# Where the split weights begin in SBUF: 64 instead of 128 bytes modulo 256

## The chip, the cores and the metric

The kernel runs on one core of a Trainium2 chip. The metric is the device time of one execution in microseconds (us). TensorE (PE in the profile) multiplies a *standing* operand, loaded ahead by a weight load of its own (PEld), with a *moving* operand that streams through it column by column. VectorE is DVE, ScalarE is ACT, GpSimd is POOL, SyncE is SP. The operands of TensorE lie in SBUF, 128 partitions wide; what this document calls a place is the byte address within a partition, taken modulo 256.

## The reference, cut to what matters

One decoder layer on 256 tokens with a width of 1024, all in float32:

```
h = RMSNorm(x);  proj = h @ w_in           # q, k/v of three branches, gates, MoBA q/k/v, merge gates
y_A = native sparse attention(proj);  y_B = block-sparse attention(proj)
x = x + (sig(g_A) * (y_A @ w_up_nsa) + sig(g_B) * (y_B @ w_up_moba)) @ w_out
x = x + relu(RMSNorm(x) @ w_ff1)**2 @ w_ff2
out = RMSNorm(x)
```

`w_in` has 4888 columns, `w_ff1` is 1024 x 4096 and `w_ff2` is 4096 x 1024, so nearly all the work is matrix products with weights that are read once.

## The kernel before

**Chunks.** All weights come as 60 chunks of at most 128 x 2048 float32 (`CHUNKS`, L20): the four of k/v (`kva`, `kvb`, whose pieces are 384 and 408 columns), eight of q and MoBA q/k/v, eight of the merge gates (`gm`), four of the up projections, four of `wout`, 16 of `ff1` and 16 of `ff2`. SyncE loads a chunk into a `raw` tile.

**Split.** `split` (L102) makes two tiles of a chunk: `whi` is the chunk rounded to the fast format `float32r` (ACT, L114), `wlo` is the rest `raw - whi` (DVE, L116). Activations are split the same way (`hTh`/`hTl`, `yTh`/`yTl`, `mxh`/`mxl`, `h2h`/`h2l`, `sqh`/`sql`). A product is then three matmuls (`mm3`, L240): high by high, high by low, low by high, added up in PSUM. The pool `wp` holds three buffers each of `raw`, `whi` and `wlo`; a buffer comes free when the last matmul that reads it is done.

**Which operand stands.** `xstat` (L245) lets the activations stand and the weights move, mostly 512 columns at a time; the input projection uses it. The up projections and `ff2_mms` (L955) do the same. `wstat` (L260) lets the weights stand and moves the activations, 256 columns at a time; `wout` and `ff1` use it. So the same buffers `whi` and `wlo` serve as moving operands in one stage and as standing ones in another.

**ff2 by seven products.** For the six chunks in `SEVEN` the four block products of `ff2` are replaced by seven products of sums (`seven_mms`, L968). Sums of weight blocks are formed by DVE in the `raw` tile (`t_sums`, L887) and split into `th` and `tl` (`t_hi`, `t_lo`), which move; sums of activations (`sh`, `sl`, `sxh`, `sxl`) stand.

**The order.** It is written out by hand: `run_slot` (L223) emits the matmuls of a slot and, at given shares of it, the splits, loads, evacuations and attention steps of that slot. The engines run their queues in this order and wait for each other by semaphores.

**Places.** Every buffer has a fixed place that follows from the sizes of the tiles allocated before it; some tiles are only there as gaps, and some operands are slices that begin a few elements into their tile. In the kernel before, the places modulo 256 are these:

| product | moving operand, place | standing operand, place | columns that move |
|---|---|---|---|
| kva | whi/wlo, 128 | hT, 128 | 384 |
| kvb, pieces 0 to 3 of a chunk | whi/wlo, 128, 224, 64, 160 | hT, 128 | 408 |
| q, qm, km, vm, gm | whi/wlo, 128 | hT, 128 | 512 |
| up projections | whi/wlo, 128 | yT, 128 | 512 |
| wout | mx, 64 | whi/wlo, 128 | 256 |
| ff1 | h2, 64 | whi/wlo, 128 | 256 |
| ff2 | whi/wlo, th/tl, 128 | sq, s, sx, 128 | 512 |
| ff2, last 24 matmuls | whi/wlo, 128 | sq, 128 | 256 |

The pieces of a kvb chunk are 408 x 4 = 1632 bytes apart, which is why they have four places; all other pieces are multiples of 256 bytes.

Of the kernel before, what the change touches and what calls it, by code (L numbers as in the profile page):

```python
# [9 lines left out]
F32R = mybir.dt.float32r  # L10
# [22 lines left out]
C_Q, C_QM, C_KM, C_VM, C_GM, C_UPN, C_UPM, C_WOUT, C_FF1, C_FF2 = (  # L33
    4, 6, 8, 10, 12, 20, 22, 24, 28, 44)
# [7 lines left out]
def hybrid_layer(ctx: ExitStack, tc: tile.TileContext, firstd, gxd, w, w1c, small, const, gf, out):  # L42
# [4 lines left out]
    wp = ctx.enter_context(tc.tile_pool(name="wp", bufs=3))  # L47
# [36 lines left out]
    raw, hi, lo = {}, {}, {}  # L84

    def seven(c):
        return c >= C_FF2 and c - C_FF2 in SEVEN

    def raw_tile(c):
        raw[c] = wp.tile([128, 2048], F32, name="raw")  # L90

# [5 lines left out]
    def load(c):  # L97
        if c < NCH:
            raw_tile(c)
            load_part(c, 0, 1)  # L100

    def split(c, part, parts=2, which=""):  # L102
        if c >= NCH:
            return
        n = CHUNKS[c][2]
        if part == 0 and c not in hi:
            hi[c] = wp.tile([128, 2048], F32R, name="whi")
            lo[c] = wp.tile([128, 2048], F32R, name="wlo")
        a, b = part * n // parts, (part + 1) * n // parts
        if seven(c):  # L110
            a, b = ((0, 512), (1024, 2048))[part]
        v = raw[c][:, a:b] if c else raw0[:, part]
        if which != "l":
            act.activation(hi[c][:, a:b], v, AF.Copy)  # L114
        if which != "h":
            dve.tensor_tensor(lo[c][:, a:b], v, hi[c][:, a:b].bitcast(F32),  # L116
                              op=ALU.subtract)
# [39 lines left out]
    for k in range(4):  # L157
        c0, c1 = (16 + 640 * k if k else 0), 16 + 640 * k + 640
        nc.sync.dma_start(g0x[:, c0:c1], firstd[:, c0:c1])
    raw_tile(1)  # L160
    arrived(0, raw[1])
    load_part(1, 0, 1)
    arrived(1, gx[:, 16 + 1024:])
    load_x(16 + 1024, 16 + 2048)
    raw_tile(2)
    arrived(2, raw[2])
    load_part(2, 0, 1)
# [17 lines left out]

    def act_pair(name, o):
        return (cp.tile([128, 2048 + e], F32R, name=name + n, tag="act" + n.upper())[:, o:o + 2048]
                .rearrange("p (k q) -> p k q", k=8) for n, e in (("h", 128), ("l", 16)))

    hTh, hTl = act_pair("hT", 16)  # L190

    def h_part(kt):
# [77 lines left out]
    def split_events(c, hs, ls):  # L270
        for i in range(2):
            at(hs[i], split, c + 2, i, 2, "h")
        for i in range(2):
            if ls[i] <= 1:
                at(ls[i], split, c + 2, i, 2, "l")
        if ls[1] <= 1 and not seven(c + 2):
            at(max(ls) + 0.05, load, c + 5)
# [304 lines left out]
    for kt in range(4):  # L582
        h_part(kt)
        split(0, kt, 4)
# [36 lines left out]
    for sec, c0, n in groups:  # L621
# [6 lines left out]
        for i in range(2):  # L628
            c = c0 + i
# [57 lines left out]
    for g in range(4):  # L687
        accs = [acc_tile(), acc_tile()]
        for i in range(2):
            c = C_GM + 2 * g + i  # L690
# [9 lines left out]


    mxh, mxl = act_pair("mx", 0)

    def upn_evac(t, i, acc):
# [26 lines left out]
    for sec, c0, kind, evac in (("upn", C_UPN, "n", upn_evac), ("upm", C_UPM, "m", upm_evac)):  # L731
        for i in range(2):
            c = c0 + i
# [44 lines left out]
    FB = {}  # L778
# [45 lines left out]
    for i in range(4):  # L824
        c = C_WOUT + i
# [33 lines left out]
    SS, TT = {}, {}  # L859
# [6 lines left out]
    def s_sums(i, r):  # L866
        if not SS:
            FB["p"].tile([128, 40], F32, name="gap3")
            for n, e in (("h", 128), ("l", 16)):
                SS[n] = cp.tile([128, 2048 + e], F32R, name="s" + n, tag="act" + n.upper())  # L870
                SS[n + "x"] = FB["p"].tile([128, 384], F32R, name="sx" + n)
        j = SEVEN.index(i)
        for n in "hl":
            SS[i, n] = (SS[n][:, 16 + 384 * j:400 + 384 * j] if j < 5 else SS[n + "x"])
        S = [FB["scr"][:, 128 * a:128 * a + 128] for a in range(4)]
        A = [[r[:, k, 128 * t:128 * t + 128] for k in range(2)] for t in range(2)]
        for o, x, y, op in ((0, A[1][0], A[1][1], ALU.add), (2, A[0][0], A[1][0], ALU.subtract),
                            (1, S[0], A[0][0], ALU.subtract), (3, A[0][1], S[1], ALU.subtract)):
            dve.tensor_tensor(S[o], x, y, op=op)
# [13 lines left out]
    def t_hi(c, a):  # L893
        if a == 0:
            for n in "hl":
                TT[n] = FB["p"].tile([128, 2176 if n == "h" else 2096], F32R, name="t" + n, tag="h2" + n)[:, 0:2048]
        v = slice(1024 * a, 1024 * a + 1024)
        act.activation(TT["h"][:, v], raw[c][:, v], AF.Copy)  # L898

# [6 lines left out]
    def ff1_evac(i, outs, whole):  # L906
        r = FB["p"].tile([128, 2, 256], F32, name="ur", bufs=2)
        rf = r.rearrange("p a q -> p (a q)")
        h, l = (FB[n][:, 2 * i:2 * i + 2, :].rearrange("p a q -> p (a q)") for n in ("sqh", "sql"))
        if whole is None:  # L910
            for m in range(2):
                act.activation(r[:, m], outs[m], AF.Relu)
        else:
            act.activation(rf, whole, AF.Relu)
        dve.tensor_tensor(rf, rf, rf, op=ALU.mult)
        act.activation(h, rf, AF.Copy)  # L916
        dve.tensor_tensor(l, rf, h.bitcast(F32), op=ALU.subtract)  # L917
        if i in SEVEN:
            s_sums(i, r)
# [8 lines left out]
    for i in range(16):  # L928
        c = C_FF1 + i
# [112 lines left out]
    for i in range(15):  # L1042
        c = C_FF2 + i
# [8 lines left out]
        if i + 2 in SEVEN:  # L1052
            at(0.62, t_sums, c + 2)
            at(0.65, t_hi, c + 2, 0)
            at(0.66, t_hi, c + 2, 1)
# [116 lines left out]
```

## Time and profile before

| | |
|---|---|
| time, median of 2 runs | 376.62 us (376.49 to 376.75) |
| span of the profiled execution, first to last instruction | 374.1 us |
| time outside the span (difference of the two) | 2.5 us |
| mean granted TensorE clock | 0.997 |
| PE, matmuls in the span | 365.5 us busy, 2388 records |
| DVE / ACT busy | 294.9 us / 219.9 us |
| HBM read | 65.47 MB |

The views used below are: the page itself; the table by stretches (for each stretch of the span its length, and the busy time of each engine with the number of instructions); the chain of waits (the work that ended last, in order of time: start, length, what); the groups of instructions; and the timeline (start, length, engine, line, operation, output and inputs, shape). In a row of the timeline a matmul's length includes its way through the array, which overlaps the next one; the *pace*, from one start to the next, is what counts for time.

### The profile page before, as it was taken

The numbers are of one execution on the slowest core, as the hardware profiler recorded it, in microseconds if no ns is written. First come the engines' busy times: TensorE is split into PE (matmuls) and PEld (weight loads), VectorE is DVE, ScalarE is ACT, GpSimd is POOL, SyncE is SP. The second block draws the span as 40 slices with busy tenths as digits, with TensorE's granted clock in tenths as the row PEclk, the third lists the DMA queues.
The fourth block names the chain that finished last, engine by engine and source line by source line (L and its number), as shares of the span: only waits on it lengthen the run. The fifth ranks groups of instructions, "written<-read, shape, count | busy, mean of one in ns | idle before, by whom it ended". The sixth has DMA issues, their size and how long they took to land.

```text
span 374.1 us, 6002 instructions
## 1 busy us (share of the span) xinstructions
PE 365.5 (98%) x2388; PEld 320.9 (86%) x2388; DVE 294.9 (79%) x476; ACT 219.9 (59%) x383; POOL 6.1 (2%) x18
## 2 busy tenths in 40 slices
PE   8999999999999999999999999999999999999993
PEld 7987778878888788778999999999998888888883
DVE  4878888896966869766867688787778879999685
ACT  6966465767747667344455566666664785555412
POOL 2020000000000000000000000000000000000000
PEclk9999999999999999999999999999999999999998
DMA  8996445334533335550675556556655535655202
GB/s 278 366 380 249 142 182 197 112 114 127 189 135 115 112 122 192 155 207 1 223 286 190 185 190 217 156 191 226 209 153 201 203 136 163 231 199 207 100 0 112
DMA packets 10539, 66.89 MB, mean 179 GB/s; under 512 B 1168, under 2 KB 1680, under 8 KB 3216
## 3 DMA queue, kind: packets, MB, share of 16 engines
q1 hardware_dynamic: 10080, 65.61, 50.1%
q10 hardware_dynamic: 432, 0.92, 0.6%
q8 instruction: 18, 0.29, 0.3%
q14 instruction: 9, 0.07, 0.1%
HBM read 65.47 MB, written 1.05 MB: 178 GB/s over the span
## 4 chain that ended last, share of the span: by engine, by line
PE 83%; DVE 7%; ACT 4%; DMA 3%; issue 2%; POOL 1%; SPq 0%; POOLq 0%; ACTq 0%; DVEq 0%
PE acc L238 53%; PE o L238 13%; PE P L238 4%; PE qacc L238 3%; PE yb L238 2%; DVE wlo L116 2%; ACT whi L114 2%; DMA raw<-in_kva_dram 2%; DMA g0x<-in_first_dram 1%; DVE x L988 1%; PE Sa L529 1%; PE Sb L529 1%; PE Sa L238 1%; PE Sb L238 1%; PE tp L319 1%
## 5 line engine op out<-in xcount | busy, mean ns | idle before, releaser
L114 ACT ACTIVATE whi<-raw 128x1024 fp32r<-128x1024 f32 (+3 forms) x124 | 118.4, 984 | 53.2 <-PE acc L238 33.7
L116 DVE TENSOR_TENSOR wlo<-raw,whi 128x1024 fp32r<-128x1024 f32 (+3 forms) x124 | 136.2, 1130 | 13.6 <-ACT whi L114 13.5
L238 PE MATMUL acc<-h2h,whi 128*128 128x256 f32 x256 | 70.7, 276 | 0.0
L238 PE MATMUL acc<-h2l,whi 128*128 128x256 f32 x256 | 70.7, 276 | 0.0
L238 PE MATMUL acc<-h2h,wlo 128*128 128x256 f32 x256 | 70.7, 276 | 0.0
L238 PE MATMUL acc<-whi,hTh 128*128 128x512 f32 (+1 forms) x128 | 51.0, 399 | 0.2 <-DVE kml L338 0.2
L238 PE MATMUL acc<-wlo,hTh 128*128 128x512 f32 (+1 forms) x128 | 50.7, 396 | 0.0
L238 PE MATMUL acc<-whi,hTl 128*128 128x512 f32 (+1 forms) x128 | 49.7, 388 | 0.0
L238 PEld LDWEIGHTS acc<-h2h,whi 128*128 128x128 f32 x256 | 48.0, 188 | 0.0
L238 PEld LDWEIGHTS acc<-h2l,whi 128*128 128x128 f32 x256 | 48.0, 188 | 0.0
L238 PEld LDWEIGHTS acc<-h2h,wlo 128*128 128x128 f32 x256 | 48.0, 188 | 0.0
L238 PE MATMUL o<-whi,sqh 128*128 128x512 f32 (+1 forms) x86 | 33.1, 385 | 0.0
L238 PE MATMUL o<-whi,sql 128*128 128x512 f32 (+1 forms) x86 | 33.0, 384 | 0.0
L238 PE MATMUL o<-wlo,sqh 128*128 128x512 f32 (+1 forms) x86 | 33.0, 384 | 0.0
L238 PEld LDWEIGHTS acc<-whi,hTh 128*128 128x128 f32 x128 | 24.3, 190 | 6.6 <-issue 1.3
L238 PEld LDWEIGHTS acc<-whi,hTl 128*128 128x128 f32 x128 | 24.3, 190 | 4.2
L238 PEld LDWEIGHTS acc<-wlo,hTh 128*128 128x128 f32 x128 | 24.3, 190 | 4.1 <-DVE wlo L116 0.3
L898 ACT ACTIVATE th<-raw 128x1024 fp32r<-128x1024 f32 x12 | 12.7, 1062 | 19.2 <-DVE raw L891 19.2
L917 DVE TENSOR_TENSOR sql<-ur,sqh 128x512 fp32r<-128x512 f32 x16 | 11.1, 693 | 11.2 <-ACT sqh L916 11.2
L238 PEld LDWEIGHTS o<-whi,sql 128*128 128x128 f32 x86 | 16.2, 188 | 3.2
L238 PEld LDWEIGHTS o<-wlo,sqh 128*128 128x128 f32 x86 | 16.2, 188 | 3.2
L238 PEld LDWEIGHTS o<-whi,sqh 128*128 128x128 f32 x86 | 16.1, 188 | 3.1
(318 smaller groups left out, 645.2 us busy)
## 6 DMA issues: line engine op xcount, KB each, us to landing
raw<-in_ff_dram SPq DMA_DIRECT2D x32, 1024.0 KB, 4.9
raw<-in_gm_dram SPq DMA_DIRECT2D x8, 1024.0 KB, 4.8
raw<-in_wout_dram SPq DMA_DIRECT2D x4, 1024.0 KB, 5.1
raw<-in_q_dram SPq DMA_DIRECT2D x2, 1024.0 KB, 5.8
raw<-in_qm_dram SPq DMA_DIRECT2D x2, 1024.0 KB, 7.5
raw<-in_km_dram SPq DMA_DIRECT2D x2, 1024.0 KB, 6.1
raw<-in_vm_dram SPq DMA_DIRECT2D x2, 1024.0 KB, 4.8
raw<-in_upn_dram SPq DMA_DIRECT2D x2, 1024.0 KB, 4.8
```

The costliest lines, as they stand in the source:

```text
L114: act.activation(hi[c][:, a:b], v, AF.Copy)
L116: dve.tensor_tensor(lo[c][:, a:b], v, hi[c][:, a:b].bitcast(F32), op=ALU.subtract)
L238: pe.matmul(o, l, r, start=start, stop=stop, skip_group_check=True)
L319: pe.transpose(tp[:, j * 256 + t * 128:j * 256 + t * 128 + 128], src[:, t, (2 * i + j) * 128:(2 * i + j + 1) * 128], ident)
L529: pe.transpose(S[x][:, j, c:c + 128], P[:, 2 * x + j, c:c + 128], ident)
L898: act.activation(TT["h"][:, v], raw[c][:, v], AF.Copy)
L917: dve.tensor_tensor(l, rf, h.bitcast(F32), op=ALU.subtract)
L988: add = lambda o, v, r: dve.scalar_tensor_tensor(o, v, r, o, op0=ALU.mult, op1=ALU.add)
```

## The change

The split weights get other places. `part_tile` allocates each `whi` and `wlo` tile 64 columns (256 bytes) longer and returns a slice of 2048 columns of it: from column 0 for `wout` and `ff1`, where the weights stand (place 128 as before), and from column 48 (192 bytes) for all others, where they move (128 + 192 = 320, place 64). `th` and `tl` are moved by the same 48 columns within their tiles. To leave room, the tile of `hTh`, `mxh` and `sh` shrinks by 64 columns. As the sizes change by multiples of 256 bytes, no other operand of any engine gets another place modulo 256. The pieces of kvb come to 64, 160, 0 and 96. On every engine the instructions, their order and their waits are the same as before.

```
+    def part_tile(name, c):
+        o = 0 if C_WOUT <= c < C_FF2 else 48
+        return wp.tile([128, 2048 + 64], F32R, name=name)[:, o:o + 2048]
+
...
         if part == 0 and c not in hi:
-            hi[c] = wp.tile([128, 2048], F32R, name="whi")
-            lo[c] = wp.tile([128, 2048], F32R, name="wlo")
+            hi[c], lo[c] = part_tile("whi", c), part_tile("wlo", c)
...
     def act_pair(name, o):
         return (cp.tile([128, 2048 + e], F32R, name=name + n, tag="act" + n.upper())[:, o:o + 2048]
-                .rearrange("p (k q) -> p k q", k=8) for n, e in (("h", 128), ("l", 16)))
+                .rearrange("p (k q) -> p k q", k=8) for n, e in (("h", 64), ("l", 16)))
...
-            for n, e in (("h", 128), ("l", 16)):
+            for n, e in (("h", 64), ("l", 16)):
                 SS[n] = cp.tile([128, 2048 + e], F32R, name="s" + n, tag="act" + n.upper())
...
             for n in "hl":
-                TT[n] = FB["p"].tile([128, 2176 if n == "h" else 2096], F32R, name="t" + n, tag="h2" + n)[:, 0:2048]
+                TT[n] = FB["p"].tile([128, 2176 if n == "h" else 2096], F32R, name="t" + n, tag="h2" + n)[:, 48:2096]
```

## The prediction

> **What bounds the kernel now.** I read the page first. One engine is busy nearly all of the time:
>
> ```profile
> span 374.1 us, 6002 instructions
> PE 365.5 (98%) x2388; PEld 320.9 (86%) x2388; DVE 294.9 (79%) x476; ACT 219.9 (59%) x383; POOL 6.1 (2%) x18
> ```
>
> PE has 8.6 us free in the whole span, so a change that only alters how fast operands are read can pay only through the pace of the matmuls. The table by stretches says where PE has no gap at all (columns: stretch, length, then busy us and number of instructions for PE, PEld, DVE, ACT, POOL):
>
> ```profile
> core 0: us, PE busy (x) PEld busy (x) DVE busy (x) ACT busy (x) POOL busy (x), PEclk, DMA share, GB/s
> 24.20:74.50 50.30, 50.30 (x325) 40.03 (x324) 41.78 (x106) 29.81 (x62) 0.00 (x0) 1.00 0.54 194
> 74.50:84.00 9.50, 9.33 (x68) 7.09 (x66) 8.90 (x15) 6.05 (x16) 0.00 (x0) 1.00 0.34 112
> 84.00:160.60 76.60, 76.57 (x467) 62.30 (x468) 58.29 (x92) 47.12 (x112) 0.00 (x0) 1.00 0.44 149
> 283.00:320.00 37.00, 37.00 (x173) 30.83 (x172) 31.94 (x39) 23.49 (x30) 0.00 (x0) 1.00 0.51 178
> ```
>
> In 24.2 to 74.5, 84.0 to 160.6 and from 283 on, PE never waits, and DVE has room: 41.78 of 50.30, 58.29 of 76.60, 31.94 of 37.00. In 74.5 to 84.0 DVE is nearly as full as PE (8.90 of 9.50). The chain of waits says who sets the end in between:
>
> ```profile
> 23.66 0.55 PE tp L366 x3
> ...
> 74.51 1.06 ACT whi L114
> ...
> 83.38 0.61 DVE kml L338
> 84.03 4.61 PE acc L238 x19
> ...
> 160.63 1.07 ACT whi L114
> ...
> 176.72 106.25 PE acc L238 x935
> 282.97 8.18 PE o L238 x36
> ...
> 351.49 1.07 ACT whi L114
> 352.58 2.36 DVE wlo L116 x2
> ...
> 364.06 0.17 DVE fst L1020
> ```
>
> Before 23.66 it runs through loads, ACT, DVE and POOL. From 24 to 74.5 it is PE, to 84.0 ACT and DVE, to 160.6 PE, to about 176 mixed, to 283 PE in wout and ff1 (whose places don't change), to 351.5 PE in ff2, and then DVE and ACT to the end.
>
> **The pace and its constant part.** The timeline gives starts; from the first and the last of a run comes the pace. First 384 columns, both operands at place 128 (9 steps apart), then 512 columns at 128 and 128 (45 steps):
>
> ```profile
> 8.24 0.33 PE L238 MATMUL acc<-whi,hTl 128*128 128x384 f32 x1
> 9.80 0.33 PE L238 MATMUL acc<-whi,hTl 128*128 128x384 f32 x1
> ...
> 330.62 0.39 PE L238 MATMUL o<-whi,sl 128*128 128x512 f32 x1
> 340.82 0.39 PE L238 MATMUL o<-whi,sl 128*128 128x512 f32 x1
> ```
>
> 1.56/9 = 173.3 ns and 10.20/45 = 226.7 ns. The difference, 53.4 ns for 128 columns, is 0.417 ns a column; what is left is 173.3 - 160.0 = 13.3 ns and 226.7 - 213.3 = 13.4 ns, the same at both widths. So a matmul at 128/128 costs its columns plus a constant of 13.3 ns. Now 256 columns, in ff1 (moving at 64, standing at 128; 55 steps) and in the last matmuls of ff2 (128 and 128; 17 steps):
>
> ```profile
> 199.74 0.28 PE L238 MATMUL acc<-h2h,wlo 128*128 128x256 f32 x1
> 205.97 0.28 PE L238 MATMUL acc<-h2h,whi 128*128 128x256 f32 x1
> ...
> 365.56 0.28 PE L238 MATMUL o<-whi,sqh 128*128 128x256 f32 x1
> 367.60 0.28 PE L238 MATMUL yb<-whi,sql 128*128 128x256 f32 x1
> ```
>
> 6.23/55 = 113.3 ns against 2.04/17 = 120.0 ns; less 106.7 for the columns, 6.6 against 13.3. The second is the constant of the wider matmuls; the first, with the moving operand 64 bytes earlier in the 256, is half of it. This pair is the case for a gain: same shape, same format, same pattern of three, other places.
>
> The Trainium skill, page "TensorE: Matmul & The Clock Gate", Part 2 (what happens when you issue a matmul), says that the streaming operand and the weight load have independent SBUF read ports, so that loading the next weights takes nothing from the running matmul. By that rule the place of one against the other would not matter and the sum would be zero (the first rival); the 120.0 against 113.3 above speaks against it, unless something else differs in the tail.
>
> **The change part by part.** No instruction is added, removed or moved. What changes is the place of the moving operand, 128 to 64, in three stretches where PE sets the end. Matmuls that read the weight parts there (each of three reads one of them; these are 512 columns wide, the first stretch beginning after the last of kvb):
>
> ```profile
> 24.95:74.50 49.55, 37.47 (x113) 1.00 0.54 191
> 24.95:74.50 49.55, 22.27 (x56) 1.00 0.54 191
> 84.00:160.60 76.60, 51.12 (x161) 1.00 0.44 149
> 84.00:160.60 76.60, 31.96 (x80) 1.00 0.44 149
> 283.00:351.50 68.50, 67.00 (x296) 1.00 0.52 184
> ```
>
> These rows are the table by stretches for the tiles `whi` and `wlo` alone (twice) and, in ff2, for PE's line L238 alone. If 512 columns go from a constant of 13.3 to 6.7 ns, a pace of 220.0, the gain is 6.67 ns for each of 113 + 56 = 169, 161 + 80 = 241 and 296, together 706: 1.13 + 1.61 + 1.97 = 4.71 us.
>
> Counted at nothing are four places, with these rows for two of them (`whi`, `wlo`, then all engines):
>
> ```profile
> 74.50:84.00 9.50, 5.43 (x16) 1.00 0.34 112
> 74.50:84.00 9.50, 3.20 (x8) 1.00 0.34 112
> 351.50:367.70 16.20, 16.20 (x84) 13.87 (x82) 13.79 (x22) 5.44 (x11) 0.56 (x1) 1.00 0.08 31
> ```
>
> The 384 and 408 columns before 24 us lie beside the chain of loads, ACT, DVE and POOL. In 74.5 to 84.0 PE would only wait longer for `kml`, which DVE begins at 83.38; without that cover the 16 + 8 matmuls are worth 0.16 us. After 351.5 the chain is DVE from 352.58 on; the 84 matmuls there are worth 0.56 us. The last up projections after 160.6 stand behind the ACT and DVE steps from 160.63. A shift is passed on at the borders: ACT at 74.51, 160.63 and 351.49 splits into a buffer that PE frees, so it starts earlier by what PE has gained. With the two counted covers open the gain would be 4.71 + 0.16 + 0.56 = 5.4 us.
>
> What could be late next is DVE in ff2, where a faster PE asks for `tl` sooner:
>
> ```profile
> 312.73 2.44 DVE L902 TENSOR_TENSOR tl<-raw,th 128x1024 fp32r<-128x1024 f32 x2
> 316.11 0.39 PE L238 MATMUL P<-tl,sqh 128*128 128x512 f32 x1
> ```
>
> `tl` is done at 315.17 and used at 316.11, 0.94 us to spare; in ff2 PE gains by then 33.1/68.5 of its 296 x 6.67 ns, 0.95 us, so next to nothing is lost, unless DVE is held up further. ACT and DVE write the weight parts at 64 instead of 128 bytes; no row separates that price, and both have room in the three stretches, so I take zero. Forecast: 376.62 - 4.71 = 371.9 us, in the profiled execution a span of 369.4 against 374.1. (The median lies 2.5 us above the span; I take that as unchanged.) This case's own range is 371.0 (the covers open, and the up projections too) to 372.7 (0.8 us lost again to DVE).
>
> **The rivals.**
>
> *No change, 376.6 us.* The 113.3 ns of ff1 may be paced by the weight loads, and 13.3 ns may be what any wide stream costs. For it: 226.7 is exactly twice 113.3. Against it: 384 columns would then take 1.5 times 113.3, 170.0, and they take 173.3. Also for it, and this is the strongest row against my forecast, 408 columns at place 128 (9.97 to 11.08, 6 steps) and at place 64 (12.20 to 13.32, 6 steps):
>
> ```profile
> 9.97 0.34 PE L238 MATMUL kvbacc<-whi,hTh 128*128 128x408 f32 x1
> 11.08 0.35 PE L238 MATMUL kvbacc<-whi,hTh 128*128 128x408 f32 x1
> ...
> 12.20 0.35 PE L238 MATMUL kvbacc<-whi,hTh 128*128 128x408 f32 x1
> 13.32 0.35 PE L238 MATMUL kvbacc<-whi,hTh 128*128 128x408 f32 x1
> ```
>
> 1.11/6 = 185.0 and 1.12/6 = 186.7 ns: place 64 gains nothing here. I hold against it that 1632 bytes are not a multiple of 256, so that these streams end and begin at shifting places, which no 512-column stream does.
>
> *Slower, 377.8 to 381.3 us.* If the 408-column rows are the ones that carry over, place 64 costs a moving stream 186.7 - 185.0 = 1.7 ns more: 706 x 1.7 = 1.2 us, 377.8. If the constant moves by a whole step the other way, to 20 ns, it is 706 x 6.67 = 4.7 us, 381.3. It decides as soon as 512 columns at 64/128 pace above 226.7 ns. Against it stands ff1, whose stream at 64 is never seen slower than the one at 128.
>
> *A larger gain, about 368 us.* If ff1 is held at 113.3 by its weight loads, the stream at 64 could have any constant from 0 to 6.6, since a 512-column matmul hides the load. With none, 706 x 13.3 = 9.4 us would go, 367.2. Nothing shows a constant below 6.6. The skill's same page, section on the back-to-back issue gap, gives 2.5 ns beside the columns for a lone stream, 215.8 ns at 512 columns; by it the gain would be 706 x 10.9 = 7.7 us, 368.9. The trace shows 226.7.
>
> **How the numbers follow.** The forecast gets 0.50: the pair 113.3/120.0 is clean, but it is at another width and its moving operand is another tile. No change gets 0.30, for the 408 columns. Slower gets 0.12, the larger gain 0.08. The range 370.9 to 377.0 holds the forecast's own range and no change (0.80), and leaves the other two out. Two per cent, about what a measurement tells from no change, is 7.5 us: only the larger gain passes it, and only with at least 10.7 of the 13.3 ns gone, so faster 0.05; slower by more than 384.1 us would need over 10 ns a matmul, 0.02; within 0.93.
>
> **What would show it.** In the changed kernel 45 steps of ff2 take 9.90 us instead of 10.20 (pace 220.0); the last 256-column matmuls pace at 113.3, not 120.0; ff1 stays at 113.3; ff2 from its first matmul to the `whi` of 351.49 is 2.0 us shorter; PE still shows no wait in the three stretches. If the last 256-column matmuls reach 113.3 and the 512 stay at 226.7, the constant is not the same thing at both widths and the first rival holds. If the paces are as said but the span falls by less than 4 us, a cover or DVE took it, and the chain will show DVE rows where PE stood. A pace above 226.7 would make the sign wrong.

## The result, and the profile after

The changed kernel takes **381.03 us** (median of 2 runs, 380.97 to 381.09) against 376.62 us before: 1.0107 times as long, with an interval of 1.0067 to 1.0148. That is 4.41 us more where the prediction had 4.71 us less. (A ratio given with an interval is not the quotient of the two medians, which is 1.0117 here; on 376.62 us the interval is 2.5 to 5.6 us.)

The head of the page of the changed kernel (busy time, share and instructions of each engine):

```profile
span 379.3 us, 6002 instructions
PE 369.9 (98%) x2388; PEld 320.2 (84%) x2388; DVE 295.1 (78%) x476; ACT 219.9 (58%) x383; POOL 6.3 (2%) x18
```

PE is busy 369.9 - 365.5 = 4.4 us longer with the same 2388 matmuls; DVE and ACT did not change by more than 0.2 us. So the matmuls themselves are slower. Which ones, the timeline of the changed kernel says (start, length, operation; its lines are 3 higher than before, L241 is the old L238). First 512 columns in ff2, moving at 64 and standing at 128 (45 steps lie between the two rows), then 256 columns in ff1, whose places the change leaves at 64/128 (105 steps), then the last 256-column matmuls of ff2, now at 64/128 too (23 steps):

```profile
330.33 0.39 PE L241 MATMUL P<-th,sqh 128*128 128x512 f32 x1
340.83 0.39 PE L241 MATMUL P<-th,sqh 128*128 128x512 f32 x1
...
198.85 0.28 PE L241 MATMUL acc<-h2h,whi 128*128 128x256 f32 x1
210.75 0.28 PE L241 MATMUL acc<-h2h,whi 128*128 128x256 f32 x1
...
370.24 0.28 PE L241 MATMUL o<-whi,sqh 128*128 128x256 f32 x1
372.85 0.28 PE L241 MATMUL yb<-whi,sql 128*128 128x256 f32 x1
```

10.50/45 = **233.3 ns** for 512 columns (226.7 before), 11.90/105 = 113.3 ns in ff1 (unchanged), 2.61/23 = 113.5 ns in the last ones (120.0 before). The same two places make 256 columns faster and 512 columns slower. Less the 0.417 ns a column, the constant of the 512-column matmul went from 13.3 to 20.0 ns, not to 6.7.

Where the time came in, the chain of waits shows. These are rows of before that the prediction did not show, and then the changed kernel's:

```profile
25.85 3.45 PE qacc L238 x15
...
299.05 6.80 PE o L238 x30
...
362.61 0.67 DVE x L1004
```

```profile
24.83 0.55 PE tp L369 x3
...
27.01 3.50 PE qacc L241 x15
...
76.18 1.06 ACT whi L117
...
85.70 4.70 PE acc L241 x19
...
179.81 2.21 PE acc L241 x17
...
286.06 8.39 PE o L241 x36
...
302.50 7.00 PE o L241 x30
...
355.00 12.61 PE o L241 x54
367.63 0.76 DVE x L1007
...
369.18 0.17 DVE fst L1023
```

The chain of the changed kernel no longer passes through the two `whi` that the prediction quotes at 160.63 and 351.49 us; it stays with PE there. The timeline still has them; in brackets stands how long ACT was idle before, and for whom:

```profile
163.57 1.06 ACT L117 ACTIVATE whi<-raw 128x1024 fp32r<-128x1024 f32 x1 [4.54 <-PE acc L241]
...
356.48 1.06 ACT L117 ACTIVATE whi<-raw 128x1024 fp32r<-128x1024 f32 x1 [2.89 <-PE o L241]
```

Set against the rows that the prediction quotes, the lag of the changed kernel grows like this:

| point | before | after | lag | grown by |
|---|---|---|---|---|
| first `tp` of PE | 23.66 | 24.83 | 1.17 | 1.17 |
| `whi` (ACT) at the end of the input stage's first part | 74.51 | 76.18 | 1.67 | 0.50 |
| `acc` after `kml` | 84.03 | 85.70 | 1.67 | 0.00 |
| `whi` (ACT) in the up projections | 160.63 | 163.57 | 2.94 | 1.27 |
| first wout matmul after `mxl` | 176.72 | 179.81 | 3.09 | 0.15 |
| first ff2 matmul | 282.97 | 286.06 | 3.09 | 0.00 |
| `whi` (ACT) of ff2's last splits | 351.49 | 356.48 | 4.99 | 1.90 |
| last `fst` (DVE) | 364.06 | 369.18 | 5.12 | 0.13 |

The 1.17 us at the start are not the change: they arise in the chain of loads, ACT, DVE and POOL, and that start differs from one execution to the next (`qacc` x15 begins at 25.85 and 27.01 us here, and between 26.00 and 27.21 in the profiles of the experiments below; at 27.03 in the one of `ff1` at distance 0, whose split weights are where they were before). Of the rest, 0.50 + 1.27 + 1.90 = 3.67 us lies in the three stretches that the prediction named, and 0.15 + 0.13 = 0.28 us in two that it counted at nothing (the last up projections after 160.6, and the time after 351.5). There is none in 74.5 to 84.0 (ACT and DVE) and none from 176.7 to 283, in wout and ff1. Together that is 3.95 us, within the interval of the measured 4.41. Thirty matmuls of ff2 take 7.00 us instead of 6.80, 6.67 ns each; fifteen of the input stage take 3.50 instead of 3.45, only 3.3 ns each.

### The profile page after: what moved, and what is told of

Read it like the earlier page. It is cut to its first block, busy times and chain, and to the rows that moved or that the text cites. A ratio compares the mean times of both kernels' runs of the same rounds, so it can differ in the third digit from the quotient of the medians.

```text
span 379.3 us, 6002 instructions
## 1 busy us (share of the span) xinstructions
PE 369.9 (98%) x2388; PEld 320.2 (84%) x2388; DVE 295.1 (78%) x476; ACT 219.9 (58%) x383; POOL 6.3 (2%) x18
## 4 chain that ended last, share of the span: by engine, by line
PE 87%; DVE 3%; ACT 3%; DMA 2%; issue 2%; POOL 1%; POOLq 0%; ACTq 0%
PE acc L241 54%; PE o L241 17%; PE P L241 4%; PE qacc L241 3%; PE yb L241 2%; DMA raw<-in_kvb_dram 2%; ACT whi L117 1%; DVE wlo L119 1%; PE Sa L532 1%; PE Sb L532 1%; PE Sa L241 1%; DMA g0x<-in_first_dram 1%; PE Sb L241 1%; PE tp L322 1%; PE tp L241 1%
## 5 line engine op out<-in xcount | busy, mean ns | idle before, releaser
L241 PE MATMUL acc<-h2h,whi 128*128 128x256 f32 x256 | 70.7, 276 | 0.0
L241 PE MATMUL acc<-h2l,whi 128*128 128x256 f32 x256 | 70.7, 276 | 0.0
L241 PE MATMUL acc<-h2h,wlo 128*128 128x256 f32 x256 | 70.7, 276 | 0.0
L241 PE MATMUL acc<-whi,hTh 128*128 128x512 f32 (+1 forms) x128 | 51.3, 401 | 0.2
L241 PE MATMUL acc<-wlo,hTh 128*128 128x512 f32 (+1 forms) x128 | 51.1, 399 | 0.1
L241 PE MATMUL acc<-whi,hTl 128*128 128x512 f32 (+1 forms) x128 | 50.0, 390 | 0.0
L241 PEld LDWEIGHTS acc<-h2h,whi 128*128 128x128 f32 x256 | 48.1, 188 | 0.0
L241 PEld LDWEIGHTS acc<-h2l,whi 128*128 128x128 f32 x256 | 48.1, 188 | 0.0
L241 PEld LDWEIGHTS acc<-h2h,wlo 128*128 128x128 f32 x256 | 48.1, 188 | 0.0
L241 PE MATMUL o<-whi,sqh 128*128 128x512 f32 (+1 forms) x86 | 33.5, 390 | 0.0
L241 PE MATMUL o<-wlo,sqh 128*128 128x512 f32 (+1 forms) x86 | 33.4, 389 | 0.0
L241 PE MATMUL o<-whi,sql 128*128 128x512 f32 (+1 forms) x86 | 33.4, 389 | 0.0
L241 PEld LDWEIGHTS acc<-whi,hTh 128*128 128x128 f32 x128 | 24.2, 189 | 7.0 <-issue 1.3
L241 PEld LDWEIGHTS acc<-wlo,hTh 128*128 128x128 f32 x128 | 24.2, 189 | 4.9 <-DVE wlo L119 0.7
L241 PEld LDWEIGHTS acc<-whi,hTl 128*128 128x128 f32 x128 | 24.2, 189 | 4.6
L920 DVE TENSOR_TENSOR sql<-ur,sqh 128x512 fp32r<-128x512 f32 x16 | 11.1, 693 | 11.2 <-ACT sqh L919 11.2
L241 PEld LDWEIGHTS o<-whi,sqh 128*128 128x128 f32 x86 | 16.1, 187 | 3.8
L241 PEld LDWEIGHTS o<-whi,sql 128*128 128x128 f32 x86 | 16.1, 187 | 3.8
L241 PEld LDWEIGHTS o<-wlo,sqh 128*128 128x128 f32 x86 | 16.1, 187 | 3.7
```

What stands on the lines that cost most here:

```text
L241: pe.matmul(o, l, r, start=start, stop=stop, skip_group_check=True)
```

## The experiments

**All pairs of places, matmuls alone.** This kernel computes none of the layer: after two loads it runs blocks of 24 matmuls, one block for each pair of places, with every other engine idle. In the names `m.s.` the letters a, b, c, d are the places 0, 64, 128, 192 of the moving and the standing operand.

```
+    for b, (n, m, s, c) in enumerate(BLOCKS):      # columns, moving place, standing place, standing columns
+        o = ((m - pm) % 256) // 4
+        q = ((s - pst) % 256) // 4
+        for j in range(24):
+            nc.tensor.matmul(acc[0:c, 0:n], sta[:, q + 128 * (j % 16):...], mov[:, o + n * (j % k):...], ...)
```

> A kernel that does nothing but matmuls (blocks of 24, each with its own standing slice), after its two operands are loaded and rounded; it computes none of the layer. One block for each pair of places (moving m, standing s) at 512, 256 and 384 columns. Theory P (the pace is made by the two reads of TensorE alone and depends on places and width): the paces of the two kernels come back with every other engine idle: 512 columns 226.7 ns at 128/128 and 233.3 at 64/128; 256 columns 120.0 and 113.3; 384 columns 173.3 at both. Theory E (writes of ACT and DVE or transfers share the banks with the reads): with those engines idle the paces at 64/128 and 128/128 are equal, and nearer to the bare columns (213.3 and 106.7).

The timeline of this kernel has a row for each block (x24); the time from one row's start to the next one's is that of 24 matmuls. 512 columns and then 256:

```profile
49.82 5.62 PE L50 MATMUL mbsb<-mov,sta 128*128 128x512 f32 x24
55.28 5.76 PE L50 MATMUL mbsc<-mov,sta 128*128 128x512 f32 x24
60.88 5.74 PE L50 MATMUL mbsd<-mov,sta 128*128 128x512 f32 x24
...
77.53 5.62 PE L50 MATMUL mcsc<-mov,sta 128*128 128x512 f32 x24
82.99 5.76 PE L50 MATMUL mcsd<-mov,sta 128*128 128x512 f32 x24
...
127.80 2.89 PE L50 MATMUL mbsc<-mov,sta 128*128 128x256 f32 x24
130.53 3.00 PE L50 MATMUL mbsd<-mov,sta 128*128 128x256 f32 x24
...
139.03 3.03 PE L50 MATMUL mcsc<-mov,sta 128*128 128x256 f32 x24
141.90 2.99 PE L50 MATMUL mcsd<-mov,sta 128*128 128x256 f32 x24
```

At 512 columns 64/128 takes 5.60 us (233.3 ns each) and 128/128 takes 5.46 (227.5 with its first few; its last twelve pace at 226.7). At 256 columns it is the other way round, 2.73 us (113.8) against 2.87 (119.6). So the paces of both kernels at 256 and 512 columns are there with ACT, DVE and the DMA queues at rest, and a contention with them is not needed for the loss. The 384 columns missed what was expected, 173.3 ns at both pairs: 64/128 paced at 174.8, 128/128 at 173.3. Over all 16 pairs of 512 columns, the last twelve of each block pace like this:

| moving against standing place | pairs | 512 columns | 256 columns |
|---|---|---|---|
| equal | 0/0, 64/64, 128/128, 192/192 | 226.7 | 120.0 to 120.3 |
| 64 below | 64/128, 0/64, 128/192, 192/0 | 233.3 | 113.3 at 64/128, 117.8 at the others |
| 64 above | 192/128, 64/0, 128/64, 0/192 | 228.8 to 228.9 | 117.8 |
| 128 apart | 0/128, 64/192, 128/0, 192/64 | 231.7 to 232.8 | 118.3 to 118.8 |

At 512 columns the distance of the two places decides to within about 1 ns, and distance 0, what the kernel before has, is the best. At 256 columns the distance alone does not: of the four pairs that are 64 below, only 64/128 has 113.3. The kernel ends with 512 columns over 64 standing ones at place 128: the moving places 0, 64, 128 and 192 pace at 229.6, 231.2, 230.0 and 228.3 ns, so there the places still differ, but by about 3 ns, where 128 standing columns at the same place differ by 6.7. The Trainium skill, page "TensorE: Matmul & The Clock Gate", Part 2, has independent read ports for the stream and the weight load; if that made them free of each other, all 16 pairs would pace alike, and they do not.

**Only ff2 moved.**

```
-        o = 0 if C_WOUT <= c < C_FF2 else 48
+        o = 48 if c >= C_FF2 else 0
```

> Only ff2 (whi, wlo, th, tl) moves from place 64; the input and up projections as before. Theory P: 296 matmuls of 512 columns cost 6.67 ns more up to the last splits, and the 60 after them too where PE then sets the end, the last 24 of 256 columns 6.67 ns less: 1.97 + 0.40 - 0.16 = 2.2 us at most, 378.6 to 378.8. Rival (the later tiles' addresses modulo 512 or more, or the longer tiles, make it): about the whole 4.4 us stays, 381.

379.08 us against 376.77: 1.0073 times (1.0043 to 1.0102), by the medians 2.31 us more. Its chain of waits has the input stage as before and ff2 as in the changed kernel:

```profile
27.21 3.43 PE qacc L241 x15
...
304.90 7.00 PE o L241 x30
```

The size is as expected to within 0.5 us. The profiled execution itself took 383.52 us, and that was not expected; the section on the hardware comes back to it.

**Only the input stage and the up projections moved.**

```
-        o = 0 if C_WOUT <= c < C_FF2 else 48
+        o = 48 if c < C_WOUT else 0
...
-                ... tag="h2" + n)[:, 48:2096]
+                ... tag="h2" + n)[:, 0:2048]
```

> Only the input and the up projections move from place 64; ff2 as before. Theory P: 410 matmuls on the chain cost 6.67 ns more: 2.7 us, 379.3; together with the ff2 part about the whole difference. Rival: as in the ff2 part, the whole 4.4 us or none of it.

379.27 us, as expected; 1.0049 times (1.0024 to 1.0073). The chain has the mirror image of the last one:

```profile
27.05 3.50 PE qacc L241 x15
...
302.17 6.80 PE o L241 x30
```

By the medians the two halves add to 2.31 + 2.50 = 4.8 us, which agrees with the 4.4 of the whole within their intervals.

**The sizes alone.** The tiles get their new lengths, but all slices begin at 0, so every operand keeps its old place modulo 256.

```
-        o = 0 if C_WOUT <= c < C_FF2 else 48
+        o = 0
...
-                ... tag="h2" + n)[:, 48:2096]
+                ... tag="h2" + n)[:, 0:2048]
```

> The tiles are 64 columns longer as in the changed kernel, but every slice begins at column 0: all places modulo 256 as before, all addresses as far apart as in the changed kernel. Theory P: 376.6, no difference. Rival (distance between tiles, or places modulo 512): 378 to 381.

376.91 us, 0.9994 times (0.9957 to 1.0031): no change, as expected. Other addresses do nothing that this interval (1.6 us less to 1.2 us more) would show, as long as the places modulo 256 stay.

**Finer distances, and few standing columns.** Again matmuls alone, none of the layer: distances in steps of 8 bytes (512 columns) and 16 bytes (256 columns), then 32 and 8 standing columns, then places 256 bytes away. In the names `d` is the distance in bytes by which the moving place lies above the standing one, `c` the standing columns, `s` the standing place modulo 512.

```
+BLOCKS = ([(512, d, 128, 128) for d in range(0, 256, 8)]
+          + [(256, d, 128, 128) for d in range(0, 256, 16)]
+          + [(512, d, c, 128) for c in (32, 8) for d in (0, 64, 128, 192)]
+          + [(512, d, 128, 384) for d in (0, 192, 256, 448)]
+          + [(512, d, 128, 64) for d in (0, 192)])
```

> The kernel of nothing but matmuls again, now with the moving operand 0 to 248 bytes above the standing one in steps of 8 (512 columns) and of 16 (256 columns), the standing one at 128; then 32 and 8 standing columns instead of 128; then both operands moved on by 256 bytes. Theory D (the distance of the two places decides, and what makes it is the load of the next weights reading beside the stream): 0 and 256 give 226.7 at 512 columns, 192 and 448 give 233.3, and with 32 or 8 standing columns the paces at all four distances fall together and nearer to the bare 213.3. Rival S (the constant belongs to the stream alone): 8 standing columns pace as 128 do. A distance with a pace below 226.7 at 512 columns, or below 113.3 at 256, would be a better place than either kernel has; none is expected at multiples of 64 bytes.

Its timeline, one row for each block of 24, for 8 standing columns and for the standing place 384:

```profile
268.07 5.71 PE L49 MATMUL xed0c8s128e<-mov,sta 128*8 128x512 f32 x24
273.62 5.72 PE L49 MATMUL xfd64c8s128e<-mov,sta 128*8 128x512 f32 x24
279.18 5.72 PE L49 MATMUL xgd128c8s128e<-mov,sta 128*8 128x512 f32 x24
284.74 5.72 PE L49 MATMUL xhd192c8s128e<-mov,sta 128*8 128x512 f32 x24
290.29 5.60 PE L49 MATMUL xad0c128s384e<-mov,sta 128*128 128x512 f32 x24
295.73 5.76 PE L49 MATMUL xbd192c128s384e<-mov,sta 128*128 128x512 f32 x24
301.33 5.62 PE L49 MATMUL xcd256c128s384e<-mov,sta 128*128 128x512 f32 x24
306.79 5.76 PE L49 MATMUL xdd448c128s384e<-mov,sta 128*128 128x512 f32 x24
```

With 8 standing columns all four distances take 5.55 or 5.56 us, 231.5 ns each, and with 32 it is much the same (231.4 to 231.7 in the last twelve): the distance counts where 128 columns are loaded, less where 64 are (the kernel of all pairs), and hardly below. But the constant does not go away with the load: 231.5 lies between the 226.7 of distance 0 and the 233.3 of 64/128. A load of 128 columns at the right distance makes the stream *faster* than one of 8. Half of that was expected otherwise: the four distances did fall together, but not towards the 213.3 ns of the columns alone. With 128 standing columns at place 128, distance 0 is the best of all 32 at 512 columns (226.7); the next are 228.9 (64 above) and 230.0 (48 above), and the worst is 238.3 (168 above). At 256 columns two of sixteen reach 113.3 (192 and 112 above), the others 116.7 to 120.0. The last four rows show that 256 bytes more change nothing: 5.44 and 5.46 us at distances 0 and 256, and 5.60 between the starts of `xbd192c128s384e` and the next.

**Both at 64.** The moving parts stay at 64 as in the changed kernel, and the activations that stand (`hT`, `yT`, `sq`, `s`, `sx`) go to 64 as well. Gap tiles are resized with them (not shown), so that what lies behind keeps its place.

```
-    hTh, hTl = act_pair("hT", 16)
+    hTh, hTl = act_pair("hT", 0)
...
-            SS[i, n] = (SS[n][:, 16 + 384 * j:400 + 384 * j] if j < 5 else SS[n + "x"])
+            SS[i, n] = (SS[n][:, 384 * j:384 + 384 * j] if j < 5 else SS[n + "x"])
```

> The changed kernel with the standing activations (hT, yT, sq, s, sx) at 64 too, so that the distance is 0 again but both places are new. Theory D (distance): 512 columns pace at 226.7 as before the change and the time is that of the kernel before, 376.6. Rival A (place 64 is bad for a moving operand of 512 columns): 233.3, 381.0.

377.14 us against 377.17, 0.9985 times (0.9964 to 1.0007). The whole loss is gone, with the weights at the changed kernel's place; the chain of waits has ff2's thirty at 6.80 us again:

```profile
300.53 6.80 PE o L241 x30
```

It is not place 64 that costs, but that the standing operand stayed at 128.

**The moving parts at 192.**

```
-        o = 0 if C_WOUT <= c < C_FF2 else 48
+        o = 0 if C_WOUT <= c < C_FF2 else 16
...
-                ... tag="h2" + n)[:, 48:2096]
+                ... tag="h2" + n)[:, 16:2064]
```

> The changed kernel with the moving weights at 192 instead of 64, the standing activations at 128: distance 64 instead of 192. By the block 192/128 of the kernel of matmuls alone (228.9 ns on the mean): 2.2 ns x 706 = 1.6 us over the kernel before, 378.2. Rival A': 192 is as bad as 64, 381.

ff2 does what the matmuls alone foretold, 6.87/30 = 229.0 ns. But the median is 381.68 us, 1.0088 times (1.0047 to 1.0128), 3.5 us over the expected 378.2 and near the 381 of the rival, though ff2 does not pace as the rival has it (233.3). Its ten times lie in two groups, three at 377.2 to 378.4 and seven at 381.2 to 382.6. The profiled execution is one of the seven, and its rows tell what made it long: ff2, and then ff1, 99 steps, in the chain and the timeline of this kernel:

```profile
304.02 6.87 PE o L241 x30
```

```profile
200.04 0.28 PE L241 MATMUL acc<-h2h,whi 128*128 128x256 f32 x1
211.70 0.28 PE L241 MATMUL acc<-h2h,whi 128*128 128x256 f32 x1
```

ff1 paces at 11.66/99 = 117.8 ns instead of 113.3, at the same places, 64/128, and from its first matmuls to its last. Over the 768 matmuls of ff1 and the 166 of wout that follow its last wait that is 4.4 ns each, 4.1 us. The lower group agrees with what was expected. That the other six of the upper group are of the same kind is likely from their times, but they left no trace.

**ff1 at distance 0.** The kernel before, with the moving operands of wout and ff1 (`mx`, `h2`) at 128 instead of 64. One gap tile shrinks by as much (not shown).

```
-    mxh, mxl = act_pair("mx", 0)
+    mxh, mxl = act_pair("mx", 16)
...
-            ... name="h2" + n, tag="h2" + n)[:, 48:2096]
+            ... name="h2" + n, tag="h2" + n)[:, 64:2112]
```

> The kernel before with the moving activations of wout and ff1 (mx, h2) at 128 instead of 64: distance 0 at 256 columns. By the block 128/128 at 256 columns: 120.0 instead of 113.3 ns for 960 matmuls, 6.4 us slower, 383.0. Rival (the 120.0 of the last 24 matmuls of the kernel before has another cause): 376.6.

382.79 us, as expected; 1.014 times (1.0102 to 1.0177). The timeline of ff1 (99 steps) gives 11.88/99 = 120.0 ns:

```profile
199.84 0.28 PE L238 MATMUL acc<-h2h,whi 128*128 128x256 f32 x1
211.72 0.28 PE L238 MATMUL acc<-h2h,whi 128*128 128x256 f32 x1
```

So the pair on which the prediction stood, 113.3 against 120.0, was the places, as it said. But it was a fact about 256 columns, and about 64/128 rather than about every pair 64 apart.

**What picks ff1's pace.** Matmuls alone (and six waits for ACT), none of the layer. Every block comes after 16 matmuls of 512 columns (`pre`); only the way into it differs. In a name the number after `n` is the width of one matmul in between, the number after `g` the width that ACT evacuates while PE waits.

```
+        m = int(e[1:])
+        if e[0] == "g":
+            nc.scalar.activation(gt[:, 0:m], pre[:, 0:m], AF.Copy)
+            nc.tensor.matmul(warm[:, 0:m], sta[:, 0:128], gt[:, 0:m], ...)
+        elif m:
+            nc.tensor.matmul(warm[:, 0:m], sta[:, 0:128], mov[:, 0:m], ...)
```

> This kernel only has matmuls (and, in six places, an ACT step that PE waits for); it computes none of the layer. It asks why ff1, with the same places 64/128 and 256 columns, paced at 113.3 ns in most profiles but at 117.8 ns in those of the two kernels with only ff2's parts moved and with the parts at 192. Each block is a long run of one kind of matmul, always after 16 of 512 columns at 128/128 (226.7 ns): the entry is either direct, or through one matmul of 16 to 112 columns, or through a wait for ACT of varying length. Twenty blocks have 256 columns at 64/128 (eight entries twice and four waits), six have 256 columns at 0/64, six have 512 columns at 64/128. Theory C: at 256 columns and 64 bytes below the standing operand there are two steady cycles, and how the run is entered picks one: each block is at 113.3 or at 117.8 from its first matmuls to its last, both values occur among the 20 blocks at 64/128, and the two blocks of one entry agree; 0/64 shows both values too. Rival X: something outside the matmul stream picks one for a whole execution: all 26 blocks of 256 columns agree. Rival Y: the absolute place decides and other engines disturb it: with the other engines idle all 20 blocks at 64/128 are at 113.3 and all six at 0/64 at 117.8. At 512 columns all theories expect 233.3 for each of the six.

Its timeline; a block's time runs from its row to the `pre` behind it:

```profile
37.13 8.73 PE L57 MATMUL binn16256d192s128e<-mov,sta 128*128 128x256 f32 x72
45.70 3.81 PE L42 MATMUL pre<-mov,sta 128*128 128x512 f32 x16
...
61.61 8.42 PE L57 MATMUL dinn48256d192s128e<-mov,sta 128*128 128x256 f32 x72
69.87 3.80 PE L42 MATMUL pre<-mov,sta 128*128 128x512 f32 x16
...
133.37 8.73 PE L57 MATMUL binn16256d192s128e<-mov,sta 128*128 128x256 f32 x72
141.93 3.81 PE L42 MATMUL pre<-mov,sta 128*128 128x512 f32 x16
...
157.85 8.42 PE L57 MATMUL dinn48256d192s128e<-mov,sta 128*128 128x256 f32 x72
166.10 3.80 PE L42 MATMUL pre<-mov,sta 128*128 128x512 f32 x16
```

After one matmul of 16 columns the 72 take 8.57 and 8.56 us, after one of 48 columns 8.26 and 8.25. The first few settle; the last twelve of a block pace at 117.8 in the one case and 113.3 in the other. Of the 20 blocks at 64/128, 13 hold 113.3 and 7 hold 117.8: the direct entry, 16 and 32 columns give 117.8 both times, 48 to 112 columns 113.3 both times; of the waits the shortest gives 117.8, the three longer ones 113.3. So at 64/128 there are two steady cycles and the entry picks one. That an execution as a whole is in one or the other (rival X), or that the place alone decides (rival Y), falls. One part of the winning theory falls too, and there rival Y was right: at 0/64 all six blocks held 117.8, whatever the entry. The six of 512 columns all settle at 233.3 in their last twelve.

## Why the prediction was wrong, point by point

- **The step that failed** is "If 512 columns go from a constant of 13.3 to 6.7 ns, a pace of 220.0". It took the pair of ff1 and the last matmuls (113.3 against 120.0) for a property of the places alone and carried it to twice the width. Both rows were read rightly (ff1 at distance 0 does pace at 120.0, the last matmuls at 64/128 at 113.5). But at 512 columns the same places go the other way, 226.7 to 233.3, with all else idle as well: the term of 706 x 6.67 ns had the wrong sign, a constant of 20.0 ns in place of 6.7.
- **The rows that spoke against it** were in the prediction, and were argued away: 408 columns, 185.0 ns at 128 and 186.7 at 64. They had the sign of the result, and they were the only rows in which the moving operand of a wide stream stood at two places against the same standing one. "Against it stands ff1" was an answer at another width.
- **"The same at both widths"** (13.3 and 13.4 ns at 384 and 512 columns) supported a constant free of the width at distance 0. At 64/128 there is none such: 6.7 ns at 256 columns, 14.8 at 384 with matmuls alone (174.8), 20.0 at 512.
- **The rival "Slower, 377.8 to 381.3"** named the case: its upper end was 706 matmuls at a constant of 20 ns, and 20.0 ns and 381.03 us came. It had 0.12.
- **"No change"**, for the reason that the place of the one does not matter to the other, fell with the 16 pairs. What the rival also said, that 13.3 ns may be what any wide stream costs, is nearer the truth as a floor: none of 32 distances went below it. By that the rival of a larger gain falls too, which had 512 columns below a constant of 6.6 ns.
- **Where it would show** was right in the main: the three stretches in which PE sets the end carry 3.67 of the 3.95 us, and 74.5 to 84.0, wout after `mxl` and ff1 carry none. The other 0.28 us came in where the prediction counted nothing: 0.15 in the last up projections, where the chain of before is back on PE from 166.18 us on (`acc` x14, then x13 from 169.82), and 0.13 after 351.5.
- **The size of the terms**: ff2 has 1.90 us where 1.97 was counted, the stretch from 84 us 1.27 where 241 x 6.67 = 1.61 was counted, and the first stretch 0.50 instead of 1.13. In the first the old pace was not 226.7: the fifteen of `qacc` took 3.45 us, 230.0 ns each, and only 3.3 ns a matmul were there to lose. The short matmuls in between are the likely reason. In the timeline of before, this `qacc` stream, which comes behind four transposes, takes 231 ns a matmul on the mean of eight steps from 26.15 to 28.00 us, and only then 227. In the kernel of entries, too, the first three or more of most `pre` blocks come at up to 239 ns before the block settles at 226.7. A run that leaves the short matmuls out was not made.
- **The covers**: in 74.5 to 84.0 the slower matmuls cost nothing, as ACT and DVE set the end there. The one after 351.5 us is gone: a slower PE now sets the end until 367.61, where before it was DVE from 352.58 on. DVE's last `x` ahead of `fst` begins 367.63 - 362.61 = 5.0 us later than before, so that this costs little (0.13 us by the table) beyond what ff2 had lost by then.

What stays open is why the distance matters. The runs show that it matters most with 128 standing columns, less with 64 and hardly with 32 or 8, that moving an operand on by 256 bytes changes nothing in the pairs tried, and that the pace belongs to the two operands together, not to the stream alone. They do not show the part of the chip in which this happens, nor why 256 columns follow another rule than 512.

## What to carry to other kernels

A matmul's constant depends on the width of the stream, on the two places modulo 256 together (at 512 columns on their distance) and on how many columns stand, so a pace found at one width is no price for another: measure the very shape first, in a kernel of matmuls alone. For 512 float32r columns over 128 standing ones put both operands at the same place modulo 256 (226.7 ns, the best of 32 distances); for 256 columns 64/128 (113.3 instead of 120.0, or 117.8 if the way into the stream falls the other way). And when one row of a profile has just the contrast that the change makes, it outweighs a cleaner pair that differs in size.

## What the runs showed of the hardware that was not expected

- **A stream at the same places has two steady paces.** At 64/128 and 256 columns it is 113.3 or 117.8 ns, and the way into the stream picks which, for as long as it lasts. In the profile with only ff2 moved the choice can be seen: just before PE waits for `mxl`, wout paces at 113.3 (six steps from 176.97 to 177.65 us), and behind that wait at 117.8 (nine steps, 1.06 us):

```profile
179.12 0.28 PE L241 MATMUL acc<-mxh,whi 128*128 128x256 f32 x1
...
180.18 0.28 PE L241 MATMUL acc<-mxh,whi 128*128 128x256 f32 x1
```

From there the pace holds through the rest of wout and all of ff1, 166 + 768 matmuls at 4.4 ns, 4.1 us: as much as the change itself. The profiled executions of the kernel with only ff2 moved (383.52 us, its other nine 378.25 to 380.31) and of that at 192 were at 117.8, all other profiles at 64/128 at 113.3. Why the kernel at 192 was in its slower group in seven of ten executions is not shown. One of 21 executions of the kernel before took 381.49 us, some 4 us above most of the others; it left no trace.
- **A larger load can quicken the stream.** With 8 or 32 standing columns 512 columns pace at 231.1 to 231.7 ns at each of the four distances tried, with 128 at 226.7 or at up to 238.3. The Trainium skill, page "TensorE: Matmul & The Clock Gate", section "Back-to-back issue gap", gives N/2.4 + 2.5 ns for an isolated matmul of N columns, by which one of 512 would take an estimated 215.8 ns. No block of 512 columns came below 226.7.
- **The steady constants are whole steps of 6.67 ns** where a block is regular to the nanosecond: 6.7 (113.3), 13.3 (120.0, 173.3 and 226.7), 20.0 (233.3). The 117.8 ns (11.1) and the 228.9 (15.6) are not among them, and their starts are not even: 117 to 119 ns apart in the one, 225 to 232 in the other (last twelve of a block).
